# Second products of a block inversion four at a time, low-rank low parts padded to 128 rows, and another order of parts, in a two-layer hybrid backbone

## The chip, the cores and the metric

The kernel runs on one core of one Trainium2 chip. The metric is the time of one execution on the device in microseconds, as a median of several runs. Profiles come from one execution of the same program under the hardware profiler.

## The reference

Two layers work on 256 context tokens and 256 latent tokens of width 1024. Each layer has three token mixers fed by one projection (a bidirectional RWKV-7 recurrence, a bidirectional gated linear recurrence, neighbourhood attention), a merge by sigmoid gates, and a gated feed-forward part with a small convolution. What the change touches is the recurrence of the first mixer and the low-rank maps that feed it:

```python
w_lo = jnp.tanh(w_lo)
for d in range(2):
    w_log = -jax.nn.softplus(-(p['rwkv_w0'][d] + w_lo @ p['rwkv_w_up'][d])) - 0.5
    a = jax.nn.sigmoid(p['rwkv_a0'][d] + a_lo @ p['rwkv_a_up'][d])
...
def step(S, inp):
    r_t, w_t, k_t, v_t, kk_t, a_t = inp
    sa = jnp.einsum('bhvk,bhk->bhv', S, -kk_t)
    S = (S * w_t[:, :, None, :] + sa[..., None] * (kk_t * a_t)[:, :, None, :]
         + v_t[..., None] * k_t[:, :, None, :])
    return S, jnp.einsum('bhvk,bhk->bhv', S, r_t)
```

`w_lo` and `a_lo` have 64 columns each, and there are 16 heads of 64. In layer 1, the last, only the 256 latent tokens are needed after the recurrences, so most of its projections have 256 columns where layer 0 has 512.

## The kernel before

Activations lie transposed, channels on the 128 partitions and tokens on the free axis. A dense product (`mm3`, L247 to L249) splits weight and activation into a high part in fp32r and a low part, and adds three matmuls per 128-row block: high x high, high x low, low x high. A weight tile (`wload`) is fetched from memory as wr by SyncE's queue, rounded to wh by ScalarE (L226), and its low part wl is made by VectorE or GpSimd (L229); which of the two is read from a list of zeros and ones for each kind of projection (`lo` in the table CFG). One projection of 1024 inputs is 24 matmuls. They appear as pj (input projection), pbr, wo (merge), fg, fu, fo (feed-forward). All other matmuls are in fp32 and leave two records each in the trace.

The recurrence is computed in chunks of 64 tokens, for a pair of heads at a time, eight pairs p per layer. For each pair: `rw_key` makes k, v, r and the row norms (kst, then kbc), and splits the low-rank weights lw into lh and ll; `rw_prep` forms the decay and the gate by two products each, pw and pa, where lh has 128 rows and ll is applied with 64 (L511, L512, L518, L519); `rw_gram` forms 32 matrices of 64x64 in Gm (2 directions, 8 chunks, 2 heads); `rw_rows` transposes what the recurrence needs (vt, bt); `rw_inv` inverts the two 32x32 diagonal blocks of all 32 triangular matrices by substitution on VectorE (31 steps, L660 and L662, on the tile AT); `rw_inv2` makes the remaining block of each inverse by two products, Q (L681: one 32x32 matmul for each of the 32 matrices, then a ScalarE copy per half, L682) and Q2 (L687, named Q in the trace too, then L688), and then sends part of KR into Gm by DMA; `rw_seq` walks through the eight chunks (r, sa, sp, yp, with small copies by ScalarE, VectorE and GpSimd between them); `rw_out` and `rw_out2` normalise and store, the latter in one product for all tokens or in two halves (`oy` in CFG).

```python
for g in range(2):
    ps = self.ps("q", "Q2").rearrange("p (j t) -> p j t", t=32)
    for i in range(16):
        j = 16 * g + i
        nc.tensor.matmul(ps[64:96, i, :], lhsT=T1[96:128, j, :], rhs=TT[32:64, j, 32:64], start=True, stop=True)
    nc.scalar.activation(TT[0:32, 16 * g:16 * g + 16, 32:64], ps[64:96], AF.Copy)
```

The other two mixers (`lru_*`, `attn_*`) and the gate projections (`gate`) are independent of the recurrence and are laid between its steps. The order is given by CFG, one table per layer: `order` is a string with a letter for each part of one pair (g gram, i inversion, I second part of it, v rows, o and O output, X, a, b, Y, S the linear recurrence, Q, A, P attention, 1 and 2 key and prep of the next pair, T the walk through the chunks, G one gate projection, N further ones by the list `ng`), `pri` gives parts a priority, and `sp` places the attention's steps behind marked matmuls of projections. A scheduler then puts instructions into each engine's queue by program order and these priorities; each engine takes its queue in that order.

Of the kernel before, what the change touches and what calls it, by code (L numbers as in the profile page):

```python
# [10 lines left out]
F32 = mybir.dt.float32  # L11
F32R = mybir.dt.float32r
AF = mybir.ActivationFunctionType
ALU = mybir.AluOpType
# [5 lines left out]
P = 128  # L20
# [24 lines left out]
for _n, _c in _CS:  # L45
# [6 lines left out]


CFG = [{'f1': 0,
  'ff': [40000, 12000],
  'fg': 0,
  'fi': 20000,
  'hp': 10000,
  'lo': {'1': [0],
         'G': [0, 1],  # L60
         'N': [1, 0],
         'Q': [0],
         'X': [0],
         'Y': [0, 1, 0],
         'fi': [0],
         'fo': [1, 1, 1, 0],
         'fp': [0, 1, 0],
         'm0': [0, 1],
         'm1': [0, 0, 0, 0, 1, 1],
         'st': [1],  # L70
         'wo': [0]},
  'lq': 0,
  'mb': 8,
  'na': 0,
  'nb': 0,
  'nc': 3,
  'ng': [4, 1, 1, 2, 1, 0, 2, 0, 5],
  'no': 5,
  'order': '||g|ovOiXQIa||YbGSTA|12NPB|',
  'oy': 1,  # L80
  'pe': [0, 0, 0, 0, 0, 0, 0],
  'pri': {'1': 20000,
          '2': 5000,
          'B': 400,
          'O': 5000,
          'S': 10000,
          'T': 5000,
          'a': 5000,
          'g': 1200,
          'i': 20000,  # L90
          'o': -200,
          'v': 2500},
  'prs': 0,
  'rot': 1,
  'rv': 1,
  'rw': 0,
  'sp': [0, 0, 0.04, 0.05, 0.18, 0.4, 0.59, 0.92, 0.98],
  'sq': 0,
  'st': -1,
  'sw': 1,  # L100
  'wo': [0, 25000],
  'yo': 0},
 {'f1': 0,
  'ff': [300, 600],
  'fg': 6,
  'fi': 0,
  'hp': 20000,
  'lo': {'1': [0],
         'G': [0, 1],
         'N': [0],  # L110
         'Q': [0],
         'X': [1],
         'Y': [0],
         'fi': [0, 1, 1, 0, 1],
         'fo': [0],
         'fp': [0, 0, 1, 0],
         'm0': [0],
         'm1': [0, 1, 0, 0],
         'st': [0],
         'wo': [0]},  # L120
  'lq': 0,
  'mb': 4,
  'na': 2,
  'nb': 2,
  'nc': 2,
  'ng': [7, 1, 1, 1, 1, 1, 2, 0, 2],
  'no': 5,
  'order': 'gvGiIXabYSQA12TNPoOB',
  'oy': 1,
  'pe': [0, 0, 3, 0, 0, 0, 0],  # L130
  'pri': {'1': 20000,
          '2': 10000,
          'A': -200,
          'B': 20000,
          'I': 20000,
          'N': 20000,
          'O': 20000,
          'S': 0,
          'T': 20000,
          'Y': -200,  # L140
          'b': 200,
          'g': 20000,
          'i': 20000,
          'o': 20000,
          'v': 20000},
  'prs': 0,
  'rot': 0,
  'rv': 0,
  'rw': 1,
  'sp': [0.04, 0.43, 0.47, 0.47, 0.72],  # L150
  'sq': 0,
  'st': -1,
  'sw': 0,
  'wo': [25000, 15000],
  'yo': 1}]
STEP1 = [3, 2, 1, 0, 7, 6, 5, 4]

# [1 line left out]
class Net:  # L159
# [302 lines left out]
    def rw_key(self, R, Q, p, n0):  # L462
        nc = self.nc
        T2 = self.rw_t2(R, Q)
        lw = self.wp.tile([P, 1024], F32, tag="wr", name="lw", bufs=3)[:, :640]
        nc.sync.dma_start(lw, self.ins["lora"][self.l, p])
        lh = Q.tile([P, 512], F32R, tag="lh", name="lh")
        ll = Q.tile([P, 512], F32R, tag="ll", name="ll")
        self.split(lw[:, :512], lh, ll)
        gw = R.tile([P, P], F32, tag="gw", name="gw", bufs=2)  # L470
        nc.gpsimd.tensor_copy(gw, lw[:, 512:])
        k = T2("k")
        self.shift(self.proj(8 + p), 8 + p, k, 0)
        v = T2("v")
        self.shift(self.proj(16 + p), 16 + p, v, 0)
        r = T2("r")
        self.shift(self.proj(p, n0), p, r, n0)

        sq = T2("ta")
        nc.scalar.activation(sq, k, AF.Square, scale=self.pvc("kk", p))  # L480
        st = self.ps("g", "kst")
        for T in range(4):
            nc.tensor.matmul(st[:, 2 * T:2 * T + 2], lhsT=sq[:, T * P:(T + 1) * P], rhs=self.c["hsel"],
                             start=True, stop=True)
        n1 = R.tile([P, 8], F32, tag="n1", name="n1")
        nc.vector.tensor_scalar(n1, st[:, 0:8], 1e-24, None, op0=ALU.max)
        n2 = R.tile([P, 8], F32, tag="n2", name="n2")
        nc.gpsimd.tensor_tensor(n2, n1, self.mhalf[:, 0:8], op=ALU.pow)
        pn = self.ps("g", "kbc")
        nb = T2("th")  # L490
        nc.scalar.activation(nb.rearrange("p (g v) -> p g v", v=64),
                             n2.rearrange("p (g o) -> p g o", o=1).to_broadcast([P, 8, 64]), AF.Copy)
        for T in range(4):
            nc.tensor.transpose(pn[:, T * P:(T + 1) * P], nb[:, T * P:(T + 1) * P], self.ident)
        kk = T2("kk")
        nc.vector.scalar_tensor_tensor(kk, k, self.pvc("kk", p), pn, op0=ALU.mult, op1=ALU.mult)
        return dict(p=p, lh=lh, ll=ll, k=k, kk=kk, gw=gw, v=v, r=r)

    def rw_prep(self, R, Q, u, n0):
        nc = self.nc  # L500
        T2 = self.rw_t2(R, Q)
        p, lh, ll, k, kk, r = (u[n] for n in ("p", "lh", "ll", "k", "kk", "r"))
# [5 lines left out]
        for d in range(2):  # L508
            pw = self.ps("g", "pw")
            dc = slice(d * P, (d + 1) * P)  # L510
            nc.tensor.matmul(pw, lhsT=lh[:, dc], rhs=self.wS, start=True, stop=False)  # L511
            nc.tensor.matmul(pw, lhsT=ll[0:64, dc], rhs=self.wS[0:64], start=False, stop=True)  # L512
            th = T2("th")
            nc.scalar.activation(th, pw, AF.Tanh, scale=0.5, bias=self.hw0[:, 8 * d + p:8 * d + p + 1])
            nc.scalar.activation(th, th, AF.Copy, bias=1.0)
            pa = self.ps("g", "pa")
            dc = slice((2 + d) * P, (3 + d) * P)
            nc.tensor.matmul(pa, lhsT=lh[:, dc], rhs=self.aS, start=True, stop=False)  # L518
            nc.tensor.matmul(pa, lhsT=ll[64:128, dc], rhs=self.aS[64:128], start=False, stop=True)  # L519
            ta = T2("ta")  # L520
            nc.scalar.activation(ta, pa, AF.Tanh, scale=0.5, bias=self.hw0[:, 16 + 8 * d + p:16 + 8 * d + p + 1])
            G = T2("G")
# [144 lines left out]
    def rw_inv2(self, R, u):  # L667
        nc = self.nc
        G = u["Gm"]
        A10, A0, Ap, Tf = u["inv"]  # L670
        TT = u["TT"] = u["RT"][64:128].rearrange("p (j t) -> p j t", t=64)
        T1 = Ap
        nc.gpsimd.memset(TT[32:64, :, 0:32], 0.0)
        nc.vector.transpose(T1[0:32].rearrange("p j s -> p s j"), Tf[64:96].rearrange("p t s -> p s t"))
        nc.vector.transpose(TT[0:32, :, 0:32].rearrange("p j t -> p t j"), Tf[64:96])
        nc.vector.transpose(TT[32:64, :, 32:64].rearrange("p j t -> p t j"), Tf[96:128])
        for g in range(2):
            ps = self.ps("q", "Q").rearrange("p (j t) -> p j t", t=32)
            for i in range(16):
                j = 16 * g + i  # L680
                nc.tensor.matmul(ps[96:128, i, :], lhsT=A10[:, j], rhs=T1[0:32, j, :], start=True, stop=True)  # L681
            nc.scalar.activation(T1[96:128, 16 * g:16 * g + 16, :], ps[96:128], AF.Copy, scale=-1.0)  # L682
        for g in range(2):
            ps = self.ps("q", "Q2").rearrange("p (j t) -> p j t", t=32)
            for i in range(16):
                j = 16 * g + i
                nc.tensor.matmul(ps[64:96, i, :], lhsT=T1[96:128, j, :], rhs=TT[32:64, j, 32:64], start=True, stop=True)  # L687
            nc.scalar.activation(TT[0:32, 16 * g:16 * g + 16, 32:64], ps[64:96], AF.Copy)  # L688
        if not self.cfg['f1']:
            for h in range(2):  # L690
                nc.sync.dma_start(G[0:64, 0, :, :, h], u["KR"][64 * h:64 * h + 64, 0])
# [912 lines left out]
```

## Time and profile before

| what | value |
|---|---|
| median of 3 runs | 2999.29 us (2991.41 to 3010.68) |
| the profiled execution | 2999.59 us |
| its span, first to last instruction | 2997.8 us |
| mean granted TensorE clock | 0.957 |
| TensorE, VectorE, ScalarE, GpSimd busy | 2834.2, 1964.5, 1512.0, 595.7 us |

A busy time is the union of an engine's instructions. Matmuls overlap one another in the trace, so TensorE's pace is read from the starts of successive matmuls, and its clock from the column of the granted clock, where 1.00 is 2.4 GHz and 0.50 is 1.2 GHz. In time, the mixers of layer 0 take about 80 to 1030 us, merge and feed-forward follow to 1740 us, the mixers of layer 1 reach to 2660 us, and merge and feed-forward of layer 1 end the span.

### The profile page before, as it was taken

The numbers are of one execution on the slowest core, as the hardware profiler recorded it, in microseconds if no ns is written. First come the engines' busy times: TensorE is split into PE (matmuls) and PEld (weight loads), VectorE is DVE, ScalarE is ACT, GpSimd is POOL, SyncE is SP. The second block draws the span as 40 slices with busy tenths as digits, with TensorE's granted clock in tenths as the row PEclk, the third lists the DMA queues.
The fourth block names the chain that finished last, engine by engine and source line by source line (L and its number), as shares of the span: only waits on it lengthen the run. The fifth ranks groups of instructions, "written<-read, shape, count | busy, mean of one in ns | idle before, by whom it ended". The sixth has DMA issues, their size and how long they took to land. (4 is left out here: it accounts for less than half of the span.)

```text
span 2997.8 us, 51813 instructions
## 1 busy us (share of the span) xinstructions
PE 2834.2 (95%) x20144; PEld 2263.7 (76%) x20144; DVE 1964.5 (66%) x3947; ACT 1512.0 (50%) x2917; POOL 595.7 (20%) x618
## 2 busy tenths in 40 slices
PE   7999999999999999989999998999999999989998
PEld 5777777777767677787778887777777777678898
DVE  6768777677776744475443268687778768755774
ACT  3565554556546542353333356655655665634453
POOL 2121120211202212200002211222221221212440
PEclk9999999999999999999999999999999998979899
DMA  6322122221222345755653452222222222236663
GB/s 226 94 70 74 56 89 64 72 68 53 87 69 68 106 158 182 255 184 182 218 175 92 121 172 83 65 78 77 67 72 82 64 64 78 87 104 211 219 195 115
DMA packets 159222, 344.30 MB, mean 115 GB/s; under 512 B 47488, under 2 KB 74368, under 8 KB 158976
## 3 DMA queue, kind: packets, MB, share of 16 engines
q1 hardware_dynamic: 152064, 334.69, 34.8%
q10 hardware_dynamic: 6912, 6.29, 0.7%
q8 instruction: 159, 2.61, 0.4%
q14 instruction: 87, 0.71, 0.1%
HBM read 301.08 MB, written 25.17 MB: 109 GB/s over the span
## 5 line engine op out<-in xcount | busy, mean ns | idle before, releaser
L226 ACT ACTIVATE wh<-wr 128x1024 fp32r<-128x1024 f32 (+1 forms) x402 | 420.1, 1046 | 537.4 <-PE pj L248 195.1
L247 PE MATMUL pj<-hh,wh 128*128 128x512 f32 (+1 forms) x1440 | 561.4, 391 | 22.6 <-DVE k L432 14.7
L229 DVE TENSOR_TENSOR wl<-wr,wh 128x1024 fp32r<-128x1024 f32 (+1 forms) x320 | 411.2, 1285 | 250.8 <-ACT wh L226 240.4
L249 PE MATMUL pj<-hh,wl 128*128 128x512 f32 (+1 forms) x1440 | 551.7, 384 | 8.2 <-POOL wl L229 4.1
L248 PE MATMUL pj<-hl,wh 128*128 128x512 f32 (+1 forms) x1440 | 551.3, 383 | 0.0
L247 PEld LDWEIGHTS pj<-hh,wh 128*128 128x128 f32 x1440 | 282.7, 196 | 83.0 <-issue 24.9
L249 PEld LDWEIGHTS pj<-hh,wl 128*128 128x128 f32 x1440 | 282.7, 197 | 61.8 <-issue 8.8
L229 POOL TENSOR_TENSOR wl<-wr,wh 128x1024 fp32r<-128x1024 f32 (+1 forms) x82 | 199.0, 2429 | 629.9 <-ACT wh L226 602.7
L248 PEld LDWEIGHTS pj<-hl,wh 128*128 128x128 f32 x1440 | 283.2, 197 | 47.1 <-issue 8.9
L741 POOL TENSOR_TENSOR sg<-SV,gC 64x128 f32<-64x128 f32 x192 | 114.3, 595 | 337.3 <-DVE SV L756 272.6
L660 DVE TENSOR_TENSOR itmp<-AT 128x126 f32<-128x126 f32 (+22 forms) x496 | 140.0, 282 | 11.2
L662 DVE TENSOR_TENSOR AT<-AT,itmp 128x126 f32<-128x126 f32 (+22 forms) x496 | 134.7, 272 | 10.8
L586 PEld LDWEIGHTS gram<-KR,BK 64*128 64x128 f32 x1024 | 120.5, 196 | 26.3 <-issue 13.9
L586 PE MATMUL gram<-KR,BK 64*128 64x128 f32 (+1 forms) x1024 | 136.6, 290 | 0.9 <-DVE Gm L589 0.4
L247 PE MATMUL fo<-fh,wh 128*128 128x256 f32 (+1 forms) x418 | 130.3, 312 | 0.0
L249 PE MATMUL fo<-fh,wl 128*128 128x256 f32 (+1 forms) x418 | 130.2, 311 | 0.0
L248 PE MATMUL fo<-fl,wh 128*128 128x256 f32 (+1 forms) x418 | 129.8, 310 | 0.0
L247 PE MATMUL fg<-hh,wh 128*128 128x256 f32 (+1 forms) x384 | 128.2, 336 | 1.1 <-ACT hh L403 1.1
L247 PE MATMUL fu<-hh,wh 128*128 128x256 f32 (+1 forms) x384 | 125.3, 327 | 2.7 <-DVE fgs L1356 2.0
L248 PE MATMUL fg<-hl,wh 128*128 128x256 f32 (+1 forms) x384 | 126.8, 331 | 0.0
L249 PE MATMUL fg<-hh,wl 128*128 128x256 f32 (+1 forms) x384 | 126.5, 330 | 0.0
L249 PE MATMUL fu<-hh,wl 128*128 128x256 f32 (+1 forms) x384 | 125.5, 328 | 1.0 <-DVE wl L229 1.0
(337 smaller groups left out, 6321.0 us busy)
## 6 DMA issues: line engine op xcount, KB each, us to landing
wr<-in_w_in SPq DMA_DIRECT2D x180, 512.0 KB, 3.3
aw<-in_ada_w SPq DMA_DIRECT2D x96, 512.0 KB, 4.6
wr<-in_ffn_w_in SPq DMA_DIRECT2D x96, 512.0 KB, 4.1
wr<-in_w_branch SPq DMA_DIRECT2D x48, 512.0 KB, 3.6
wr<-in_ffn_w_out SPq DMA_DIRECT2D x36, 512.0 KB, 3.6
wr<-in_w_out SPq DMA_DIRECT2D x24, 512.0 KB, 4.7
Gm<-KR SPq DMA_DIRECT2D x32, 256.0 KB, 4.3
wr<-in_ffn_w_out SPq DMA_DIRECT2D x18, 384.0 KB, 3.1
```

Source lines behind the costliest of these rows:

```text
L226: nc.scalar.activation(hi, raw, AF.Copy)
L229: eng.tensor_tensor(lo, raw, hi.bitcast(F32), op=ALU.subtract)
L247: nc.tensor.matmul(o, lhsT=a, rhs=xh[k][:, n0:n1], start=(first and k == 0), stop=False)
L248: nc.tensor.matmul(o, lhsT=a, rhs=xl[k][:, n0:n1], start=False, stop=False)
L249: m = nc.tensor.matmul(o, lhsT=b, rhs=xh[k][:, n0:n1], start=False, stop=(last and k == kt - 1))
L586: nc.tensor.matmul(ps[:, i, 0:nx], lhsT=BK[hs, d, c, :], rhs=KR[hs, 0:nx, d, c, :], start=True, stop=True)
L660: eng.tensor_tensor(tmp, Ap[:, q + 1:32, q:q + 1].to_broadcast([P, nt, ns]), Tf[:, q:q + 1, 0:2 * ns:2].to_broadcast([P, nt, ns]), op=ALU. ...
L662: eng.tensor_tensor(Tf[:, q + 1:32, 0:2 * ns:2], Tf[:, q + 1:32, 0:2 * ns:2], tmp, op=ALU.subtract)
L741: nc.gpsimd.tensor_tensor(sg[64 * h:64 * h + 64], SV[0:64, i, :, h], gC[:, :, h, i:i + 1].to_broadcast([64, 2, 64]), op=ALU.mult)
```

## The change

Three pieces of code and both tables change. The second products take four of the 32 matrices at once: the four blocks of T1 stand side by side as one stationary operand of 128 columns, the four right-hand blocks as one moving operand of 128 columns, and of the sixteen 32x32 products that come out, the four on the diagonal are copied, each by a ScalarE instruction of its own for every fourth matrix. The low parts ll are made for the 64 rows that count in each half and set to zero in the others, and are applied with all 128 rows. The tables get another order of parts, other priorities, other lists of who makes wl, and other counts of gate projections per pair (`ng` counts them at the start and behind each pair's walk; the total stays 24 per layer).

```diff
 CFG = [{'f1': 0,
...
-  'ng': [4, 1, 1, 2, 1, 0, 2, 0, 5],
+  'ng': [3, 1, 3, 2, 1, 0, 2, 0, 4],
   'no': 5,
-  'order': '||g|ovOiXQIa||YbGSTA|12NPB|',
-  'oy': 1,
+  'order': 'g||ovOXiQ||a||Yb|IGAT|12|NSPB|',
+  'oy': 0,
...
  {'f1': 0,
...
-         'fi': [0, 1, 1, 0, 1],
-         'fo': [0],
+         'fi': [1],
+         'fo': [1],
...
-  'order': 'gvGiIXabYSQA12TNPoOB',
+  'order': 'GgviXabYISQA12TPNoOB',
...
@@ rw_key
-        self.split(lw[:, :512], lh, ll)
+
+        nc.scalar.activation(lh, lw[:, :512], AF.Copy)
+        for x in range(2):
+            rs, cs = slice(64 * x, 64 * x + 64), slice(256 * x, 256 * x + 256)
+            nc.vector.tensor_tensor(ll[rs, cs], lw[rs, cs], lh[rs, cs].bitcast(F32), op=ALU.subtract)
+            nc.gpsimd.memset(ll[rs, 256 - 256 * x:512 - 256 * x].bitcast(F32), 0.0)
@@ rw_prep
-            nc.tensor.matmul(pw, lhsT=ll[0:64, dc], rhs=self.wS[0:64], start=False, stop=True)
+            nc.tensor.matmul(pw, lhsT=ll[:, dc], rhs=self.wS, start=False, stop=True)
...
-            nc.tensor.matmul(pa, lhsT=ll[64:128, dc], rhs=self.aS[64:128], start=False, stop=True)
+            nc.tensor.matmul(pa, lhsT=ll[:, dc], rhs=self.aS, start=False, stop=True)
@@ rw_inv2
-            ps = self.ps("q", "Q2").rearrange("p (j t) -> p j t", t=32)
-            for i in range(16):
-                j = 16 * g + i
-                nc.tensor.matmul(ps[64:96, i, :], lhsT=T1[96:128, j, :], rhs=TT[32:64, j, 32:64], start=True, stop=True)
-            nc.scalar.activation(TT[0:32, 16 * g:16 * g + 16, 32:64], ps[64:96], AF.Copy)
+            ps = self.ps("q", "Q2").rearrange("p (m a t) -> p m a t", a=4, t=32)
+            for m in range(4):
+                j = slice(16 * g + 4 * m, 16 * g + 4 * m + 4)
+                nc.tensor.matmul(ps[:, m], lhsT=T1[96:128, j, :].rearrange("p a t -> p (a t)"), rhs=TT[32:64, j, 32:64],
+                                 start=True, stop=True)
+            for a in range(4):
+                nc.scalar.activation(TT[0:32, 16 * g + a:16 * g + 16:4, 32:64], ps[32 * a:32 * a + 32, :, a], AF.Copy)
```

On TensorE, around the inversion of the second pair of layer 0, the order before is this (the last row begins a projection whose 24 matmuls follow; L855 and L856 are products of the linear recurrence):

```order
L247 MATMUL pj_2578<-hh_368,wh 128x512
L681 MATMUL Q<-AT,Gm 32x32 x32
L248 MATMUL pj_2578<-hl_376,wh 128x512
L249 MATMUL pj_2578<-hh_368,wl 128x512
L855 MATMUL lr<-xb,gw 128x512
L856 MATMUL li<-xb,gw 128x512
L687 MATMUL Q_2527<-RT,AT 32x32 x16
L687 MATMUL Q_2545<-RT,AT 32x32 x16
L247 MATMUL pj_2624<-hh_361,wh 128x512
L247 MATMUL pj_2916<-hh_361,wh 128x512
```

In the changed kernel, at the same pair, the rows around the first products and those around the second are these, and the 23 projection matmuls between the two pieces are not shown:

```order
L252 MATMUL pj_2450<-hh_368,wl 128x512
L865 MATMUL lr<-xb,gw 128x512
L866 MATMUL li<-xb,gw 128x512
L689 MATMUL Q<-AT,Gm 32x32 x32
L250 MATMUL pj_2556<-hh_361,wh 128x512
L250 MATMUL pj_2837<-hh_361,wh 128x512
...
L252 MATMUL pj_2837<-hh_368,wl 128x512
L695 MATMUL Q_2536<-RT,AT 128x128 x4
L695 MATMUL Q_2545<-RT,AT 128x128 x4
L251 MATMUL pj_2556<-hl_369,wh 128x512
```

The two products of the linear recurrence have moved ahead of the first products, and 25 projection matmuls stand between the first and the second products where there were two and the pair lr, li.

At the last inversion of layer 1, TensorE's order before has attention ahead of it and the merge behind it:

```order
L1080 MATMUL ao<-PT,vt 64x64 x8
L681 MATMUL Q<-AT,Gm 32x32 x32
L687 MATMUL Q_25026<-RT,AT 32x32 x16
L687 MATMUL Q_25044<-RT,AT 32x32 x16
L723 MATMUL r_25310<-SV,Gm 128x128 x2
```

The changed kernel has the same neighbours there:

```order
L1090 MATMUL ao<-PT,vt 64x64 x8
L689 MATMUL Q<-AT,Gm 32x32 x32
L695 MATMUL Q_24872<-RT,AT 128x128 x4
L695 MATMUL Q_24881<-RT,AT 128x128 x4
L733 MATMUL r_25038<-SV,Gm 128x128 x2
```

Nothing has moved into this place; only the form of the second products differs.

GpSimd's queue ends so before, with the row norm of the last residual (st_r) behind 25 weight halves:

```order
L1128 TENSOR_TENSOR M_25683<-M_25683,mth 128x256
L229 TENSOR_TENSOR wl<-wr,wh 128x1024
L276 TENSOR_TENSOR st_r<-st_m,mhalf 128x2 x2
L229 TENSOR_TENSOR wl<-wr,wh 128x1024 x25
L276 TENSOR_TENSOR st_r<-st_m,mhalf 128x2
```

In the changed kernel it ends so, with three more groups of 4 and 2 rows like the third and fourth from the end left out:

```order
L232 TENSOR_TENSOR wl<-wr,wh 128x1024 x2
L279 TENSOR_TENSOR st_r<-st_m,mhalf 128x2 x2
L232 TENSOR_TENSOR wl<-wr,wh 128x1024 x45
...
L232 TENSOR_TENSOR wl<-wr,wh 128x1024 x4
L232 TENSOR_TENSOR wl<-wr,wh 128x768 x2
L232 TENSOR_TENSOR wl<-wr,wh 128x1024
L279 TENSOR_TENSOR st_r<-st_m,mhalf 128x2
```

All 68 weight halves of layer 1's feed-forward part stand on GpSimd, and VectorE's queue has none of them.

## Rows read from the trace of the kernel before

**Rows 1.** The page's first part: busy time, share, instructions of each engine.
```profile
PE 2834.2 (95%) x20144; PEld 2263.7 (76%) x20144; DVE 1964.5 (66%) x3947; ACT 1512.0 (50%) x2917; POOL 595.7 (20%) x618
```
**Rows 2.** Busy time of each engine by stage, with granted clock and DMA.
```profile
core 0: us, PE busy (x) PEld busy (x) DVE busy (x) ACT busy (x) POOL busy (x), PEclk, DMA share, GB/s
80.00:1030.00 950.00, 925.51 (x6278) 688.69 (x6277) 704.01 (x1531) 533.10 (x1103) 183.62 (x224) 0.97 0.24 74
1740.00:2600.00 860.00, 805.37 (x5802) 632.06 (x5801) 640.34 (x1357) 512.20 (x1042) 191.48 (x246) 0.95 0.26 79
2600.00:2660.00 60.00, 45.50 (x350) 35.70 (x349) 41.34 (x115) 24.06 (x58) 5.06 (x5) 0.69 0.32 97
```
**Rows 3.** What TensorE waited for: us in total, times, longest us.
```profile
PE Q L681 <- DVE AT L674: 18.1, 12, 4.8
PE kbc L494 <- ACT th L491: 13.6, 13, 2.3
PE r L723 <- DMA Gm<-KR: 2.3, 1, 2.3
```
**Rows 4.** TensorE's timeline in layer 0: start us, us, instruction.
```profile
187.84 0.40 PE L248 MATMUL pj<-hl,wh 128*128 128x512 f32 x1
188.07 0.40 PE L518 MATMUL pa<-aS,lh 128*128 128x512 f32 x1
188.40 0.50 PE L519 MATMUL pa<-aS,ll 64*128 64x512 f32 x1
188.83 0.51 PE L249 MATMUL pj<-hh,wl 128*128 128x512 f32 x1
189.17 0.40 PE L247 MATMUL pj<-hh,wh 128*128 128x512 f32 x1
189.41 0.40 PE L248 MATMUL pj<-hl,wh 128*128 128x512 f32 x1
189.73 0.56 PE L745 MATMUL sa<-r,RT 64*64 64x64 f32 x6
190.22 0.50 PE L249 MATMUL pj<-hh,wl 128*128 128x512 f32 x1
190.56 0.39 PE L247 MATMUL pj<-hh,wh 128*128 128x512 f32 x1
```
**Rows 5.** Instructions on pw, pa, lh and ll: ns min/median/max, first and last start.
```profile
L511 PE MATMUL pw<-wS,lh x32: 388/404/628, 74.2 to 2527.1; 128*128 128x512 f32 x32
L512 PE MATMUL pw<-wS,ll x32: 491/498/792, 74.5 to 2527.5; 64*128 64x512 f32 x32
L518 PE MATMUL pa<-aS,lh x32: 387/397/632, 76.0 to 2540.0; 128*128 128x512 f32 x32
L519 PE MATMUL pa<-aS,ll x32: 491/497/792, 76.3 to 2540.4; 64*128 64x512 f32 x32
L237 DVE TENSOR_TENSOR ll<-lw,lh 128x512 fp32r<-128x512 f32 x16 | 11.0, 685 | 2.0 <-ACT lh L234 1.9
```
**Rows 6.** A GpSimd group by form: busy us, mean ns, idle before.
```profile
L709 POOL MEMSET SV<- 64x256 f32 x16 | 4.9, 308 | 7.3 <-PE yp L706 6.6 <-DVE pr L917 0.6
```
**Rows 7.** TensorE's timeline: second products at full and half clock, gram.
```profile
2101.92 2.21 PE L687 MATMUL Q<-RT,AT 32*32 32x32 f32 x64
...
1994.15 3.62 PE L687 MATMUL Q<-RT,AT 32*32 32x32 f32 x64
...
222.71 2.05 PE L586 MATMUL gram<-KR,BK 64*128 64x128 f32 x16
```
**Rows 8.** Stretches around one inversion; granted clock is the third from last.
```profile
1989.40:1991.50 2.10, 2.10 (x65) 2.09 (x64) 2.09 (x2) 0.77 (x2) 0.00 (x0) 1.00 0.00 0
1992.10:1994.10 2.00, 2.00 (x11) 1.82 (x9) 1.97 (x2) 0.20 (x2) 0.00 (x0) 0.51 0.42 86
1994.20:1997.60 3.40, 3.40 (x65) 3.40 (x64) 2.89 (x6) 1.49 (x2) 0.00 (x0) 0.50 0.51 104
```
**Rows 9.** ScalarE's copies out of Q2 and of r.
```profile
L688 ACT ACTIVATE RT<-Q x32: 567/587/597, 148.7 to 2644.4; 32x512 f32<-32x512 f32 x32
...
L728 ACT ACTIVATE r<-r 64x128 f32<-64x128 f32 x256 | 69.2, 270 | 74.2 <-PE r L723 68.8 <-ACT wh L226 0.2
```
**Rows 10.** The last inversion: TensorE's first products and their wait.
```profile
2636.85 3.61 PE L681 MATMUL Q<-AT,Gm 32*32 32x32 f32 x64 [4.75 <-DVE AT L674]
```
**Rows 11.** GpSimd's weight halves in layer 1's feed-forward part.
```profile
2817.63 3.16 POOL L229 TENSOR_TENSOR wl<-wr,wh 128x1024 fp32r<-128x1024 f32 x1 [0.18 <-ACT wh L226]
2854.05 2.41 POOL L229 TENSOR_TENSOR wl<-wr,wh 128x1024 fp32r<-128x1024 f32 x1 [5.92 <-DVE fgs L1355]
```
**Rows 12.** TensorE's timeline in layer 1's feed-forward part, 256 columns.
```profile
2839.64 0.28 PE L247 MATMUL fu<-hh,wh 128*128 128x256 f32 x1
...
2841.04 0.28 PE L247 MATMUL fu<-hh,wh 128*128 128x256 f32 x1
```
**Rows 13.** DMA issues: KB each, median us from issue to landing.
```profile
Gm<-KR SPq DMA_DIRECT2D x32, 256.0 KB, 4.3
```

More of the change, by code (lines that the diff above doesn't have):

```diff
@@ L54 @@
 CFG = [{'f1': 0,
-  'ff': [40000, 12000],
+  'ff': [40000, 0],
   'fg': 0,
-  'fi': 20000,
-  'hp': 10000,
+  'fi': 10000,
+  'hp': 20000,
   'lo': {'1': [0],
-         'G': [0, 1],
-         'N': [1, 0],
+         'G': [0, 1, 1],
+         'N': [0],
          'Q': [0],
          'X': [0],
-         'Y': [0, 1, 0],
+         'Y': [0, 0, 1, 0, 1, 0],
          'fi': [0],
-         'fo': [1, 1, 1, 0],
+         'fo': [1, 0, 1],
          'fp': [0, 1, 0],
-         'm0': [0, 1],
-         'm1': [0, 0, 0, 0, 1, 1],
-         'st': [1],
+         'm0': [1],
+         'm1': [0, 0, 1, 1],
+         'st': [1, 0],
          'wo': [0]},
   'lq': 0,
-  'mb': 8,
+  'mb': 4,
   'na': 0,
@@ L83 @@
           '2': 5000,
-          'B': 400,
+          'B': 2500,
           'O': 5000,
+          'P': 400,
           'S': 10000,
           'T': 5000,
-          'a': 5000,
+          'a': 400,
+          'b': 0,
           'g': 1200,
@@ L91 @@
           'o': -200,
-          'v': 2500},
+          'v': 20000},
   'prs': 0,
@@ L96 @@
   'rw': 0,
-  'sp': [0, 0, 0.04, 0.05, 0.18, 0.4, 0.59, 0.92, 0.98],
+  'sp': [0, 0, 0.16, 0.23, 0.24, 0.47, 0.6, 0.83, 1],
   'sq': 0,
@@ L101 @@
   'wo': [0, 25000],
-  'yo': 0},
+  'yo': 1},
  {'f1': 0,
@@ L106 @@
   'fi': 0,
-  'hp': 20000,
+  'hp': 10000,
   'lo': {'1': [0],
@@ L110 @@
          'N': [0],
-         'Q': [0],
+         'Q': [0, 0, 0, 0, 0, 1],
          'X': [1],
          'Y': [0],
-         'fi': [0, 1, 1, 0, 1],
-         'fo': [0],
-         'fp': [0, 0, 1, 0],
-         'm0': [0],
-         'm1': [0, 1, 0, 0],
+         'fi': [1],
+         'fo': [1],
+         'fp': [1, 0, 0, 0, 0, 0],
+         'm0': [0, 0, 1, 1, 1, 0],
+         'm1': [0],
          'st': [0],
@@ L122 @@
   'mb': 4,
-  'na': 2,
+  'na': 1,
   'nb': 2,
@@ L126 @@
   'ng': [7, 1, 1, 1, 1, 1, 2, 0, 2],
-  'no': 5,
-  'order': 'gvGiIXabYSQA12TNPoOB',
+  'no': 4,
+  'order': 'GgviXabYISQA12TPNoOB',
   'oy': 1,
   'pe': [0, 0, 3, 0, 0, 0, 0],
-  'pri': {'1': 20000,
-          '2': 10000,
+  'pri': {'1': 2500,
+          '2': 200,
           'A': -200,
-          'B': 20000,
+          'B': -200,
           'I': 20000,
-          'N': 20000,
+          'N': 400,
           'O': 20000,
@@ L140 @@
           'Y': -200,
-          'b': 200,
+          'a': 0,
+          'b': 2500,
           'g': 20000,
-          'i': 20000,
+          'i': 5000,
           'o': 20000,
-          'v': 20000},
+          'v': 200},
   'prs': 0,
@@ L149 @@
   'rw': 1,
-  'sp': [0.04, 0.43, 0.47, 0.47, 0.72],
+  'sp': [0.0, 0.35, 0.36, 0.55, 0.64],
   'sq': 0,
-  'st': -1,
+  'st': -2,
   'sw': 0,
-  'wo': [25000, 15000],
+  'wo': [600, 15000],
   'yo': 1}]
```

## Prediction

> **What bounds the kernel now.** I read the page first. TensorE has matmuls in flight 95% of the span, VectorE is busy 66%, ScalarE 50%, GpSimd 20% [rows 1]. The table by stage says the same of each: TensorE is 97% busy in the mixers of layer 0 (80 to 1030 us) and 94% in those of layer 1 (1740 to 2600 us); the one poor stretch is 2600 to 2660 us, 45.5 us of 60 at a mean clock of 0.69 [rows 2]. So a change pays through what TensorE issues, what it waits for, and the clock it is granted. The waits come next: the longest sum of any one cause is 18.1 us, in front of the first products of the inversion (Q, L681), for VectorE's transposes [rows 3]. The last view is the timeline, for the spacing of starts. In a run of whole-array matmuls of 512 columns one starts every 0.23 us. A matmul that uses part of the array breaks that: in rows 4 the 64-row product L519 starts 0.33 us after L518, its successor L249 0.43 us later, and the next L247 0.34 us after that. Durations hide this, since matmuls overlap; starts show it.
>
> The profiled execution took 2999.59 us, its span 2997.8, 1.8 us outside it. The median of the three runs is 2999.29 us, so the sum is made against 2999.6.
>
> **The padded low parts.** 64 matmuls (2 layers, 8 pairs of heads, 2 directions, two kinds) lose their 64-row form. The trace has them at 498 and 497 ns, against 404 and 397 ns for the 128-row products before them [rows 5]. From rows 4, each costs 0.33 + 0.43 + 0.34 = 1.10 us over three starts, where three whole-array starts cost 3 x 0.235 = 0.70: 0.40 us too much. Where the next matmul is itself of part of the array (nearly one in six of them), about half of that stays. That is 64 x 0.40 = 25.6 us at most; at one third of the gain, the excess of the 64-row start alone (0.20 x 64), 13. I take **-22 us**, with -13 to -26 as the ends. A rule of the Trainium skill speaks against this term (TensorE: Matmul & The Clock Gate, "Why this matters for your kernels"): a single 32-row matmul takes as long as one with 128 rows. By it the term is 0; the durations in rows 5 do not agree. What makes the padding: one VectorE subtract of 685 ns [rows 5] becomes two over 64x256, and GpSimd gets two memsets of 64x256, 308 ns each in the row of that size [rows 6]. In the new order both stand a whole pair ahead of the products that read them, right behind the last readers of the old content. VectorE has a third of its time free; I cost them at nothing. Without that cover it would be 16 x 0.6 = 10 us.
>
> **The second products.** Per inversion 32 products of 32x32 (64 records) become 8 of 32x128 by 128 columns (16 records). The block of 64 records lasts 2.21 us in the timeline at full clock and 3.62 us at half [rows 7]. The nearest row of the new size is the gram product, 64 rows, 128 columns: 16 records in 2.05 us [rows 7]. So 0.16 x 16 = **-3 us**; at half clock the new block would be twice as long, 0.2 us worse than the old, so the ends are 0 and -3 from work alone.
>
> What the clock adds is a term of its own. The first block (at 1989.4) runs at 1.00; behind it the granted clock falls to its lower level, 1.2 GHz, and the projections and the second block in this case run at 0.51 and 0.50 [rows 8]. Five of the 16 second blocks lie wholly there, and 1.4 us (3.62 less 2.21) comes back for each that leaves it: 7 us. The new blocks fill four times the columns of the array, and in layer 0 a projection separates them from the first block; the first block is untouched. I take **-7 us**, from 0 to -36 (the last end is a rival).
>
> The results now leave PSUM by four ScalarE copies per half in place of one. One took about 0.59 us [rows 9]; four of 128 elements, at the 270 ns of the nearest row (L728, 64x128) [rows 9], are 1.08. That is 32 x 0.49 = 16 us more of ScalarE. In layer 0, seven projection matmuls and r lie between the last second product and sa, which needs the result, about 2 us; that covers it. In the last inversion nothing lies between, but there r waits for the transfer into Gm anyhow (2.3 us, [rows 3]). I take **+1 us**; with all cover gone it is +16.
>
> **The order.** In layer 0 one more projection (24 matmuls, 24 x 0.23 = 5.5 us) now stands ahead of the first products of most inversions, and 25 matmuls between the two blocks where there were as few as two. VectorE meanwhile has 89 to 96 instruction rows from the first transpose of an inversion to the last in most pairs, where it had 93 to 104. Of the 18.1 us in rows 3, 4.75 us are the last inversion's [rows 10], whose place is unchanged. The other 13 can go; something is late elsewhere, first of all the row norm (kbc waits for ScalarE's th, 13.6 us [rows 3]), whose cover in layer 1 shrinks in places from five matmuls to two. I take **-12 us**; the ends are -19 and, as a rival, a loss.
>
> TensorE's sequence goes from whole array to part of it 491 times, before 526; 64 of the 526 were the low parts, so without them the count rises by 29. One such visit costs: from 189.41 to 190.56 us two whole starts and six sa records took 1.15 us; 0.47 are the two starts and 6 x 0.059 the records, which leaves 0.33 [rows 4]. 29 x 0.33 = 9.6 us; direct changes between two kinds of part-array products fall from 270 to 217, which gives some back. **+5 us** (0 to +10). The last inversion of layer 1 leaves TensorE idle a quarter of 2600 to 2660 us [rows 2], and 24 more projection matmuls of 256 columns move into it: 24 x 0.12 = **-3 us** (0 to -3).
>
> All 68 low halves of layer 1's weights in the feed-forward part go to GpSimd (before 26 of the 44 of the first two products and none of the last one's). One takes 2.41 us there [rows 11]; TensorE uses a weight in 2.8 us (twelve of its 24 matmuls take 1.40 [rows 12]). So TensorE stays the later one and I cost it at nothing; if each took 3.16, the longest in rows 11, it would be 68 x 0.35 = +24 us. One output product instead of two halves in layer 0 (rw_out2) streams the same columns; nothing, or up to -4. DMAs: the transfer into Gm, 4.3 us to landing [rows 13], still has over 6 us of matmuls between its release (the first products) and r everywhere but in the last inversion, as before.
>
> Sum: -22 - 3 - 7 + 1 - 12 + 5 - 3 = -41, so 2999.6 - 41 = **2958 us** after rounding down.
>
> **The rivals.** *The padding gives nothing*, as the skill's rule has it: 2958 + 22 = 2980. For it: the longer duration may be the change of rows, paid anyway at a neighbour. Against it: in rows 4 both neighbours are whole-array.
> *The order gives nothing*: waits only change their place, the two blocks stay slow, and the 29 visits cost in full: -22 - 3 + 1 + 10 = -14, so 2986. For it: before, TensorE was already 97% busy in layer 0.
> *The clock*: means of 0.97 and 0.95 over 950 and 860 us [rows 2] are 71 us of full-speed work lost; if the wide blocks bring back half, it is -36 in place of -7: 2929. Against it: the first blocks stay as they are, and the clock falls behind these.
> *The inversion comes late* (slower): VectorE carries eleven more weight halves in layer 0's mixers, which GpSimd did before, and in layer 1 the first products stand earlier in the sequence, ahead of a low-rank product. If each of the 16 waits became like the last one, 4.75 us [rows 10], they would sum to 76 us, 58 more than now, and the result is 2958 + 12 + 58 = 3028. It decides against the change once these waits pass 18 + 29 = 47 us, 2.9 per inversion. Against it: the longer cover ahead of the first products in layer 0.
>
> **How the numbers follow.** The forecast has 0.62, with 2938 to 2978 as its own range; padding for nothing 0.10, order for nothing 0.12, clock 0.08, late inversion 0.08. A measurement of this kernel tells about 1% from no change, so the bounds are 2969 and 3029. Faster: 0.85 of the forecast, the clock, a little of the order's case, 0.63. Slower: half of the late inversion, 0.04. Same: 0.33. The range, 2918 to 2992, leaves out the late inversion and the tails.
>
> **What would show it.** Right: the low products of pw and pa last 0.40 us and start 0.23 us apart; sixteen-record blocks of Q2 near 2.05 us; the wait for L674's successor under 8 us; a mean clock of 0.96 to 0.97. Wrong: low products that still start 0.33 us or more behind their partner; waits of sa for the copies out of Q2, or of the feed-forward matmuls for GpSimd's wl, of over 5 us; a first block that waits more than 2.9 us for VectorE each time; or a clock that rises by more than 0.015.

## The result, and the profile after

The changed kernel took 2970.09 us (median of three runs, 2964.05 to 2974.57) against 2999.29; the ratio on record is 0.9888 (95% interval 0.9853 to 0.9922), a little under the quotient of the two medians, 0.990. In six more runs beside other kernels it took 2977.19 us against 3001.78, a ratio of 0.9920 (0.9898 to 0.9942). By the medians that is 29 and 25 us less, by the ratios 34 and 24; the forecast was 41 less. Both times lie inside the likeliest case's own range of 2938 to 2978, at its upper end. The bound for faster, 2969 us, was just missed by both medians, although the first ratio lies more than 1% under 1.

The page's first part of the changed kernel, the execution of 2964.05 us, answers to [rows 1]:

```profile
span 2962.2 us, 50439 instructions
PE 2784.8 (94%) x19360; PEld 2241.2 (76%) x19360; DVE 1941.1 (66%) x3921; ACT 1521.7 (51%) x3005; POOL 694.0 (23%) x676
```

The table by stage, with the columns of [rows 2] (granted clock third from last), of the same execution:

```profile
80.00:1030.00 950.00, 917.67 (x6082) 691.41 (x6083) 725.88 (x1583) 544.84 (x1171) 177.72 (x231) 0.99 0.26 77
1740.00:2600.00 860.00, 794.27 (x5398) 621.64 (x5396) 648.27 (x1426) 520.99 (x1097) 199.06 (x254) 0.94 0.26 76
2600.00:2660.00 60.00, 52.39 (x459) 47.07 (x460) 31.93 (x67) 24.93 (x59) 8.66 (x14) 0.84 0.43 122
```

The gain is not spread over the span. The merge of layer 0 ends its mixers; its first matmul starts at 1087.3 us before and at 1056.0 after, 31 us sooner. From there to the end the span has 1910.5 us before and 1906.2 after: in these two profiles all but 4 us of the gain was made in the mixers of layer 0, where the granted clock rose from 0.97 to 0.99 (0.02 x 950 = 19 us of full-speed work). A second profile of the changed kernel, from the six later runs, has the merge 26 us sooner and gives 11 of them back behind it. The rows of the first two starts, from before and after:

```profile
L247 PE MATMUL pbr<-hh,wh x128: 388/389/795, 1087.3 to 1245.3; 128*128 128x512 f32 x128
```

```profile
L250 PE MATMUL pbr<-hh,wh x128: 387/390/796, 1056.0 to 1216.3; 128*128 128x512 f32 x128
```

What TensorE waited for after the change (us in total, times, longest), against [rows 3]:

```profile
PE kbc L502 <- ACT th L499: 15.3, 15, 2.1
PE Q L689 <- DVE AT L682: 10.2, 6, 5.0
PE r L733 <- DVE SV L766: 5.4, 14, 0.6
PE sa L755 <- ACT r L738: 3.3, 9, 1.4
PE pj L252 <- POOL wl L232: 1.7, 1, 1.7
PE r L733 <- DMA Gm<-KR: 1.4, 1, 1.4
PE fg L252 <- POOL wl L232: 0.9, 1, 0.9
PE fu L252 <- POOL wl L232: 0.6, 1, 0.6
```

The wait ahead of the first products fell by 8 us, and small waits of the walk (r for SV, 14 times; sa for r's copy) took the place of some of it. In all, waits alone explain little of 30 us.

The padded products start 0.24 us behind their partner and 0.22 us ahead of the next, where [rows 4] had 0.33 and 0.43:

```profile
172.03 0.40 PE L250 MATMUL pj<-hh,wh 128*128 128x512 f32 x1
172.26 0.39 PE L526 MATMUL pa<-aS,lh 128*128 128x512 f32 x1
172.50 0.39 PE L527 MATMUL pa<-aS,ll 128*128 128x512 f32 x1
172.72 0.39 PE L251 MATMUL pj<-hl,wh 128*128 128x512 f32 x1
172.95 0.39 PE L252 MATMUL pj<-hh,wl 128*128 128x512 f32 x1
```

The durations of the groups that the change touched, with the columns of [rows 5]:

```profile
L520 PE MATMUL pw<-wS,ll x32: 387/394/628, 73.4 to 2487.0; 128*128 128x512 f32 x32
L527 PE MATMUL pa<-aS,ll x32: 389/396/662, 75.0 to 2498.8; 128*128 128x512 f32 x32
L476 DVE TENSOR_TENSOR ll<-lw,lh x32: 407/421/500, 43.1 to 2419.2; 64x256 fp32r<-64x256 f32 x32
L477 POOL MEMSET ll<- x32: 302/306/428, 36.4 to 2397.4; 64x256 f32 x32
L698 ACT ACTIVATE RT<-Q x128: 264/267/274, 146.5 to 2613.1; 32x128 f32<-32x128 f32 x128
```

And one inversion of layer 0 in TensorE's timeline, then the last one of layer 1 at half clock (compare [rows 7, 10]):

```profile
255.25 2.21 PE L689 MATMUL Q<-AT,Gm 32*32 32x32 f32 x64
263.60 2.05 PE L695 MATMUL Q<-RT,AT 32*128 32x128 f32 x16
...
2604.59 3.62 PE L689 MATMUL Q<-AT,Gm 32*32 32x32 f32 x64 [5.01 <-DVE AT L682]
2608.53 3.75 PE L695 MATMUL Q<-RT,AT 32*128 32x128 f32 x16 [0.32 <-DVE RT L684]
```

The wide block takes 2.05 us, as the gram row had said, and 3.75 at half clock, 0.13 more than the narrow one: the prices of the instructions were right. Whether the pieces were worth what the sum gave them needs the experiments.

### The profile page after: what moved, and what is told of

It is laid out like the page before. It is cut to its first block, busy times and chain, and to the rows that moved or that the text cites. A ratio compares the mean times of both kernels' runs of the same rounds, so it can differ in the third digit from the quotient of the medians.

```text
span 2962.2 us, 50439 instructions
## 1 busy us (share of the span) xinstructions
PE 2784.8 (94%) x19360; PEld 2241.2 (76%) x19360; DVE 1941.1 (66%) x3921; ACT 1521.7 (51%) x3005; POOL 694.0 (23%) x676
## 5 line engine op out<-in xcount | busy, mean ns | idle before, releaser
L232 DVE TENSOR_TENSOR wl<-wr,wh 128x1024 fp32r<-128x1024 f32 (+1 forms) x286 | 359.3, 1257 | 212.0 <-ACT wh L229 186.7
L232 POOL TENSOR_TENSOR wl<-wr,wh 128x1024 fp32r<-128x1024 f32 (+1 forms) x116 | 273.5, 2366 | 537.1 <-ACT wh L229 527.2
L751 POOL TENSOR_TENSOR sg<-SV,gC 64x128 f32<-64x128 f32 x192 | 121.4, 632 | 331.4 <-DVE SV L766 267.2
L594 PEld LDWEIGHTS gram<-KR,BK 64*128 64x128 f32 x1024 | 117.5, 193 | 24.4 <-issue 10.2
L766 DVE TENSOR_TENSOR SV<-sp,sg 64x128 f32<-64x128 f32 x192 | 55.2, 288 | 118.8 <-PE sp L761 114.9
```

Source lines behind the costliest of these rows:

```text
L232: eng.tensor_tensor(lo, raw, hi.bitcast(F32), op=ALU.subtract)
L594: nc.tensor.matmul(ps[:, i, 0:nx], lhsT=BK[hs, d, c, :], rhs=KR[hs, 0:nx, d, c, :], start=True, stop=True)
L751: nc.gpsimd.tensor_tensor(sg[64 * h:64 * h + 64], SV[0:64, i, :, h], gC[:, :, h, i:i + 1].to_broadcast([64, 2, 64]), op=ALU.mult)
L766: nc.vector.tensor_tensor(SV[0:64, i + 1, :, h], pp[hs, :, h], sg[hs], op=ALU.add)
```

## The experiments

The change has three pieces: padding, wide second products, tables. Two kinds of kernel take them apart. In the first kind the scheduler is free, as in both kernels. That turned out to matter: padding leaves 98% or more of TensorE's sequence (counted by kind of product over the traces) as it was, while the wide products alone, with the old tables, leave 82%; the scheduler has 24 matmuls fewer and six copies more per inversion to place, and lays everything behind them otherwise. So in the second kind ("order held") every engine's sequence is fixed to that of a named kernel by edges that set the order of issue on each engine. No run holds a kernel to its own order, so what the holding costs by itself was not measured; in the pairs compared below, the held kernel is once the one with wide products and twice the one with narrow ones.

All results in one table. The kernels ran in three series, each on another chip and each with the kernel before; the difference is (ratio - 1) x the median of before in the same series (3001.3, 3003.9 and 3001.8 us). The medians alone would move a difference by up to 5 us.

| kernel | padding | products | tables, order | ratio to before (95%) | us |
|---|---|---|---|---|---|
| padding alone | yes | narrow | old | 0.9944 (0.9923 to 0.9964) | -17 |
| wide alone | no | wide | old | 1.0048 (1.0026 to 1.0071) | +14 |
| both codes | yes | wide | old | 1.0011 (0.9988 to 1.0034) | +3 |
| tables alone | no | narrow | new, free | 1.0012 (0.9987 to 1.0037) | +4 |
| wide, order held | no | wide | old, before's order | 1.0009 (0.9988 to 1.0030) | +3 |
| without padding | no | wide | new | 0.9949 (0.9929 to 0.9969) | -15 |
| order alone | no | narrow | new, changed kernel's order | 0.9909 (0.9887 to 0.9932) | -27 |
| narrow, order held | yes | narrow | new, changed kernel's order | 0.9879 (0.9852 to 0.9907) | -36 |
| table of layer 0 | yes | narrow | new in layer 0, old in 1 | 0.9885 (0.9858 to 0.9912) | -35 |
| one copy | yes | wide, one copy | new, changed kernel's order | 0.9893 (0.9869 to 0.9917) | -32 |
| filled wait | yes | narrow | new, changed kernel's order | 0.9872 (0.9846 to 0.9899) | -38 |
| changed kernel again | yes | wide | new | 0.9920 (0.9898 to 0.9942) | -24 |

**Padding alone.** The kernel before with this edit and the making of ll from the change:

```diff
-            nc.tensor.matmul(pw, lhsT=ll[0:64, dc], rhs=self.wS[0:64], start=False, stop=True)
+            nc.tensor.matmul(pw, lhsT=ll[:, dc], rhs=self.wS, start=False, stop=True)
...
-            nc.tensor.matmul(pa, lhsT=ll[64:128, dc], rhs=self.aS[64:128], start=False, stop=True)
+            nc.tensor.matmul(pa, lhsT=ll[:, dc], rhs=self.aS, start=False, stop=True)
```

> Before, with the padded low parts alone (old tables, narrow second products). Theory: 64 matmuls each take 0.40 us less of TensorE over three starts, about half of it in each layer: 13 to 26 us less, most likely 22, so 2977 us; the low products of pw and pa last 0.40 us. Rival, the padding gives nothing because a 64-row product costs as much as a 128-row one: 2999 us. Second rival, the gain comes back as waits because VectorE's chain of the inversion is no faster: between the two, 2985 to 2995, with the wait of Q for AT longer than 18 us.

Measured: 17 us less. TensorE's timeline of this kernel, near the place of [rows 4]:

```profile
185.62 0.40 PE L522 MATMUL pa<-aS,lh 128*128 128x512 f32 x1
185.86 0.39 PE L523 MATMUL pa<-aS,ll 128*128 128x512 f32 x1
186.09 0.40 PE L249 MATMUL pj<-hh,wl 128*128 128x512 f32 x1
186.32 0.39 PE L247 MATMUL pj<-hh,wh 128*128 128x512 f32 x1
```

Over the low products at full clock (60 of the 64 in each trace), the three steps around one, from its partner's start to that of its second successor, sum to 1.03 us on average before and to 0.74 here: 64 x 0.29 = 19 us. Timing and starts agree, so the rival "padding gives nothing" is out. The rule of the Trainium skill behind that rival (TensorE: Matmul & The Clock Gate, "Why this matters for your kernels") is given for a single 32-row matmul; for the 64-row products here, which stand among other matmuls, the trace does not agree (0.50 us long, padded 0.40). The waits ahead of the first products rose from 18.1 to 21.0 us in total, which is the second rival's sign, but small beside the gain.

**Wide products alone**, and **both pieces of code**, with the old tables and a free scheduler. The edit is that of the change in `rw_inv2`; the second adds the padding.

> Before, with the second products four at a time alone. Theory: 3 us less of work, up to 7 less through the clock, 1 more through the copies: 2990 us, at the edge of what can be told. Rival, the narrow second blocks bring much of the low clock: 36 less, 2963 us, and the time at the lower clock level falls by half. Rival on the other side, the four copies per half stand on the path (sa waits for ScalarE): 16 more, 3012 us or over 2999 in any case.

> Before, with both pieces of code (padding and wide second products) and the old tables. If the terms add: 22 + 3 + 7 - 1 = 31 less, 2968 us, which is where the changed kernel lies already, and then the new tables gave nothing. By the prediction's sum the tables are worth 10 more, so this kernel should lie 10 above the changed one, near 2980 where the changed kernel is at 2970. Rival: the new code only pays with the new tables, and this kernel stays above 2990.

Measured: +14 and +3 us. With the old tables and a free scheduler, the wide products take back what the padding gives. For the wide products alone, 3010.72 us is near the slow rival's 3012, but its sign did not come: sa's waits for ScalarE's copies of r are 1.2 us in all, 0.8 before. For both pieces the rival's number came: with the old tables the new code gives nothing.

**Tables alone.**

> The changed kernel's tables with the old code (low parts of 64 rows, narrow second products). Theory: order -12, whole-to-part visits +5, projections into the end of the mixers -3: 2989 us. Rival, the tables were fitted to the new code and alone give nothing or a loss: 2999 us or more. Rival, the tables carry most of the result because the shorter waits ahead of the first products and the clock of layer 0 come from the order: 2975 us, with layer 0's mixers 20 us or more shorter than before and layer 1's not.

Measured: +4 us, the number of the first rival; but the second rival's sign is there too. The mixers of layer 0 end 27 us sooner than before's (the merge's first matmul starts at 1060.0 us), and from there on this execution takes 45 us longer than before's. Its last inversion comes late, and the granted clock in layer 1's mixers is 0.90 where before had 0.95. Its timeline, its waits and that stage:

```profile
2657.58 3.59 PE L685 MATMUL Q<-AT,Gm 32*32 32x32 f32 x64 [13.73 <-DVE AT L678]
```

```profile
PE Q L685 <- DVE AT L678: 23.8, 8, 13.7
1740.00:2600.00 860.00, 807.51 (x5516) 631.32 (x5514) 618.05 (x1321) 497.43 (x1009) 190.47 (x236) 0.90 0.24 74
```

The late inversion is the prediction's slower rival at one place, and explains 9 of the 45 us (13.7 against 4.75 [rows 10]). The clock is the larger part: 0.05 x 860 = 43 us of full-speed work. Why it is lower is not shown, and the profiled execution was the slowest of this kernel's twelve (3017.09 us, median 3004.72). The scheduler, given narrow products, made another order of the same table: 72% of TensorE's sequence, counted as above, is that of the changed kernel.

**The order held.** The remaining kernels answer what each piece does when nothing else moves. The edit, beside the undone pieces:

```diff
+def hold(tc, nc):
+    want = json.loads(zlib.decompress(base64.b64decode(HELD)))
+    for e, v in _traced(nc).items():
...
+        for a, b in zip(seq, seq[1:]):
+            tc.add_manual_dep(b, a.name, mybir.DependencyInfo(mybir.DependencyClass.NoSync, mybir.DependencyReason.DATA), reason="held")
```

HELD is the list of places of a kernel's instructions on each engine. Where a group of four narrow products stands for one wide product, it takes that one's place, and one copy takes the place of the last of four.

> The changed kernel with the low parts back to 64 rows; its order of instructions stays nearly the same. Theory: the padding is worth here what it was worth in the old kernel, 17 to 22 us: 2987 to 2992 us, low products at 0.50 us again. Rival: part of the padding's gain in the old kernel was the granted clock and it gives half here: about 2978.

> The changed kernel with the narrow second products (32 products and one copy per half), every engine's order held to that of the changed kernel by issue-order edges, so that only the products differ. By the prediction's terms (-3 work, -7 clock, +1 copies) this is 9 us above the changed kernel: 2979. Rival: the wide products themselves are worth nothing, all of the difference came by the order that the scheduler made around them: 2970. Rival: the wide products hold the clock up: 2990 or more, with the time at the lower level up by 40 us.

> Before with the wide second products alone, every engine's order held to that of before by issue-order edges. If the 14 us that the wide products cost with the free scheduler came from the reshuffled order, this kernel is at or under before: 2990 to 2999 us (2991 by the prediction's terms). If they come from the products and their four copies themselves (copies on the path of sa), it stays at 3010.

> Before's code (low parts of 64 rows, narrow second products) with the new tables, its order held to the one the scheduler makes for the wide products. Theory: the order itself is worth 10 to 20 us, and the new tables alone gave nothing only because the scheduler made another order of them: 2980 to 2985 us. Rival: the order is worth nothing without the new code: 3000 to 3005, as with the new tables and a free scheduler. By the prediction's terms (-12 +5 -3) it is 2990.

Without padding (free, but over 99% of the sequence kept): -15 us (2985.35, between the two answers and nearer the first), where the changed kernel has -24 and -34, so padding is worth 9 to 19 here; between the two kernels with narrow products (-27, -36) it is 9. Wide products in before's order: +3 (3003.10, between the two answers), which can't be told from nothing. So 11 of the 14 us lost with the free scheduler would be its new order, although the two intervals overlap by a hair. In the changed kernel's order, narrow products are no slower than wide ones: 0.9879 against 0.9888 and 0.9920; without padding it is 0.9909 against 0.9949, intervals that overlap by a hair. Three pairs, none with a gain from the wide products. In the first the wide kernel is the held one, in the other two the narrow one, so neither a cost nor a benefit of holding can hide such a gain in all three. The expectation of 2979 for the narrow ones failed, at 2964.70.

The order alone gives 27 us, with before's code (2975.94 us, better than the 2980 to 2985 expected). Its stage, and its wait ahead of the first products:

```profile
80.00:1030.00 950.00, 919.06 (x6426) 686.03 (x6424) 726.62 (x1568) 535.25 (x1116) 172.35 (x216) 1.00 0.25 77
```

```profile
PE Q L719 <- DVE AT L712: 9.2, 6, 5.0
```

The clock in layer 0's mixers is 1.00 here, 0.97 before. This is not one execution's luck: in the five profiles with the old table of layer 0 it is 0.97 or 0.98, in the nine with the new one 0.98 once, 0.99 seven times and 1.00 once. What the order does to it is seen at one inversion of layer 0. Before, five stretches: projections, the wait, the first products, what follows, and the second products (columns of [rows 8]):

```profile
261.00:265.60 4.60, 4.60 (x22) 3.75 (x20) 4.33 (x14) 3.11 (x8) 0.00 (x0) 1.00 0.35 114
265.60:267.80 2.20, 0.43 (x3) 0.05 (x2) 2.13 (x3) 0.00 (x0) 0.00 (x0) 1.00 0.00 0
267.80:270.80 3.00, 3.00 (x64) 3.00 (x64) 2.99 (x2) 0.59 (x1) 0.00 (x0) 0.60 0.03 5
270.80:275.30 4.50, 4.50 (x9) 1.84 (x7) 1.99 (x2) 2.93 (x4) 0.00 (x0) 0.51 0.28 58
275.30:278.00 2.70, 2.70 (x67) 2.55 (x67) 0.00 (x0) 0.98 (x2) 0.31 (x1) 1.00 0.51 136
```

And the same pair in the changed kernel: projections with lr and li, the first products, a projection, the second products:

```profile
248.00:255.20 7.20, 7.20 (x29) 5.03 (x27) 7.05 (x6) 4.81 (x10) 0.00 (x0) 1.00 0.00 0
255.30:257.40 2.10, 2.10 (x66) 2.06 (x65) 2.10 (x4) 1.25 (x3) 0.00 (x0) 1.00 0.00 0
257.40:263.50 6.10, 6.09 (x27) 4.53 (x25) 2.60 (x4) 5.60 (x9) 0.62 (x1) 1.00 0.98 200
263.60:265.60 2.00, 2.00 (x18) 1.88 (x17) 2.00 (x2) 1.98 (x3) 0.56 (x1) 1.00 1.12 237
```

Before, TensorE stood still for 1.8 us and then did 64 records that use a 32x32 part of the array; the clock fell to 1.2 GHz inside that block, and the next 4.5 us, projections among them, ran at 0.51. After, the wait is covered and nothing falls. Of before's eight first blocks in layer 0, six stood more than 1.5 us behind their predecessor, and in five of these the clock fell within the block; the two others kept 1.00. In the order-alone kernel six of eight follow at once (0.52 us), and the clock fell within none of the eight (behind one of the two others it did). So the 1.8 us wait cost about 5: itself, and 3.0 x 0.40 + 4.5 x 0.49 = 3.4 for the work done at the lower clock behind it. As an estimate, five such falls are at most 17 us, and with the 9 us by which the waits shrank this is near the 27. The Trainium skill (TensorE: Matmul & The Clock Gate, "HAM oscillation — how this bites in real kernels") tells of such a second payment behind waits for transfers; the trace agrees that it is paid, and adds that here the clock still stood at 1.00 in the wait and fell in the block behind it (0.60).

It isn't a rule without exceptions. In [rows 8], from layer 1 before, the first block follows its predecessor after 0.21 us, and the clock falls behind it all the same; the one at 2097.57 us waited 1.45 us and the clock stayed at 1.00. And no run moves only lr and li ahead of the first products: that the covered wait, and not another part of layer 0's new table, steadies the clock is read from these traces and not tested by itself.

**The copies.**

```diff
             for a in range(4):
-                nc.scalar.activation(TT[0:32, 16 * g + a:16 * g + 16:4, 32:64], ps[32 * a:32 * a + 32, :, a], AF.Copy)
+                if a == 2:
+                    nc.scalar.activation(TT[0:32, 16 * g:16 * g + 16, 32:64], ps[64:96].rearrange("p m a t -> p (m a) t"), AF.Copy)
```

> The changed kernel in its own order, with one ScalarE copy per half of the second products in place of four; so the results of three of every four matrices are wrong entries, and 96 ScalarE instructions are left out. If the four copies cost what they add to ScalarE (0.49 us per half, 16 us in all), 2954; by the prediction's +1 it stays at 2969. If the kernel with narrow products is 5 us faster than the changed one because of the copies, this one is near 2964 too; if because of the wide matmuls, it stays at 2970.

Measured 2970.79 beside the changed kernel's 2977.19: between the answers for the copies and for the wide matmuls, with overlapping intervals. One wait agrees in kind: sa's for r's copy on ScalarE, 3.3 us in the changed kernel's first profile and 2.1 in its second, is 0.6 here and 0.7 with narrow products:

```profile
PE sa L793 <- ACT r L776: 0.6, 3, 0.2
```

What the four copies cost is thus some microseconds at most of the possible 16; how much, if anything, is open.

**The changed kernel again**, and **a filled wait.** The last edit adds, ahead of the last inversion's first products:

```diff
+            if g == 0 and len(UNITS) == 15:
+                for i in range(FILL):
+                    mm = nc.tensor.matmul(qp, lhsT=self.wS[:, :P], rhs=self.wS, start=True, stop=True)
```

> The changed kernel once more, for a tighter interval and beside the next three. Every theory: 2970 us, ratio to before 0.985 to 0.992.

> The kernel with the narrow second products in the changed kernel's order, with 16 extra matmuls of 128x512 that compute nothing needed in the last inversion's 5 us wait of TensorE for VectorE. They take 3.4 us at 2.4 GHz and 6.8 at 1.2. Theory: what TensorE did before sets the clock there, and with the wait filled the two blocks of that inversion run in 2.0 us in place of 3.4, and the walk behind them starts at 2.4 GHz: 3 to 8 us less than without the fill, 2957 to 2962. Rival: the clock there stays at its lower level whatever fills the wait, and the fill costs up to 2 us: 2965 to 2967.

Measured for the changed kernel: the 2977.19 us given above, a ratio of 0.9920, at the expectation's upper end. For the filled wait: 2965.09, against 2964.70 for the same kernel without the fill in another series: no difference that can be told. That is the rival's number, but not its mechanism. The timeline shows why, first without the fill, then with it:

```profile
2600.61 3.62 PE L723 MATMUL Q<-AT,Gm 32*32 32x32 f32 x64 [5.01 <-DVE AT L716]
2604.55 3.59 PE L729 MATMUL Q<-RT,AT 32*32 32x32 f32 x64 [0.32 <-DVE RT L718]
...
2598.29 4.77 PE L725 MATMUL Q<-wS 128*128 128x512 f32 x16
2603.52 2.21 PE L729 MATMUL Q<-AT,Gm 32*32 32x32 f32 x64 [0.47 <-DVE AT L717]
2607.46 3.59 PE L735 MATMUL Q<-RT,AT 32*32 32x32 f32 x64 [1.73 <-DVE RT L719]
```

The 16 extra matmuls took 4.77 us, and the first block did run at full clock (2.21 us, without the fill 3.62): at this one place only what TensorE did in the wait was changed, and the clock followed. But TensorE then waited 1.73 us for RT, where it had waited 0.32, and the second block was at half clock again. What the faster block gained was spent waiting for VectorE.

**The table of layer 0 alone**, with padding and narrow products:

> Before with the padded low parts, the new table for layer 0 and the old one for layer 1; second products narrow. Tables alone made the mixers of layer 0 27 us shorter and those of layer 1 56 us longer in the profile, and padding alone gave 17 to 20 us. If the table of layer 0 works without the wide products, the two add: 2999 - 27 - 17 = 2955 to 2965 us, under the changed kernel. Rival: the table of layer 0 needs the wide products, or the clock takes the gain back: 2975 to 2985.

Measured 2964.97 us, -35, at the upper end of the 2955 to 2965 expected. The table of layer 0 needs no wide products.

A version that beats both kernels is thus at hand: the new order or the new table of layer 0, the padding, and the old second products. In three kernels of this kind the ratios are 0.9872 to 0.9885. The filled one, in the same series as the changed kernel, was 12 us faster, with intervals (0.9846 to 0.9899 and 0.9898 to 0.9942) that only touch.

## Why the prediction was right, and where its sum was not

The time fell into the forecast's own range. The sum behind it was near in total by errors that cancel, which is luck: the order gave 17 us more than its three terms, the second products 12 to 21 less than theirs, the padding 3 to 13 less.

- **The padding, -22:** right in mechanism, somewhat large. 17 in the old order, 9 to 19 in the new one. "Nearly one in six" is right: in before's trace 9 of the 60 at full clock have a next matmul on part of the array. Too large is the 0.40 for the others: it was read where two 128x512 projection products follow, which holds for 15 of the 60, while 34 have among their next two a product that is not a projection's. The mean is 0.29. In the new order, held, the three steps fall from 1.00 to 0.68 us, 64 x 0.32 = 20 us, and 9 were measured; where the rest came back isn't settled. (Of the ends given, 0.20 a product is half of 0.40, not a third.)
- **The second products, -3, clock -7, copies +1:** wrong together. The block's length was right (2.05 us, at half clock 0.13 worse), but held in place the wide products gave between +3 and +12 us, never the -9 of these three terms. The failed step is "1.4 us comes back for each that leaves it": at an equal order the wide blocks don't keep the clock up. The mean granted clock in layer 0's mixers is 0.99 with wide and with narrow products in the changed kernel's order, and two wide second blocks of layer 1 still ran at half clock, one of them at 2608.53 us above. The rival "the clock", -36 from the wide blocks, falls with it. Whether they cost something, and if so whether it is the copies, isn't settled.
- **The order, -12, +5, -3:** 27 in place of 10. The wait ahead of the first products fell by 8 us of the 12 forecast. The failed step is to have priced a removed wait at its own length: in layer 0 before, five of the six longer waits were followed by a fall of the clock, and the work at half speed behind them cost more than the wait. The clock's gain was in the sum, but it stood at the wide blocks and not at the order. The +5 for visits and the -3 for the end of layer 1's mixers were not measured by themselves.
- **Layer 1** has half of the padded products, and no gain that can be told: behind layer 0's mixers one profile of the changed kernel is 4 us shorter than before, the other 11 longer, with clocks of 0.94 and 0.92 in layer 1's mixers where before had 0.95. But the six profiles with the old table of layer 1 range from 0.92 to 0.95 there, so these differences are within what that stage does by itself. Whether the new table of layer 1 gives or costs anything isn't settled; the kernel with the old one is as fast.
- **GpSimd's weight halves, 0:** right. The feed-forward matmuls waited 1.5 us for them. **Gm's DMA, 0:** right.
- Of the signs given ahead: 0.40 us and 0.23 apart, 2.05 us and a clock of 0.96 to 0.97 came (0.966; in the later profile 0.957, just under it); the wait of Q was 10.2 us, not under 8; none of the signs against came.
- The rival "the order gives nothing" is out by the order-alone kernel, and "the inversion comes late" didn't happen in the changed kernel, but did at one inversion, the last, in the one with its tables and the old code.

## What to carry to other kernels

Price a TensorE wait not at its length alone: look at the granted clock of the stretch behind it, here where products on a part of the array followed. Before crediting or blaming an edit in a scheduled kernel, compare the instruction order of all engines, and time the edit once with the order held; here one edit read +14 us free and +3 held, and one table +4 free and -27 held. Padding a 64-row contraction with zeros to all 128 rows, worth 9 to 19 us for 64 products here, is worth trying where such a product stands between whole-array ones.

## What the runs showed that was not expected

The granted clock differs between executions of one and the same kernel, and with it the time. Before ran 35 times in one series, from 2979.97 us at a mean clock of 0.965 to 3013.65 at 0.951; time and clock have a correlation of -0.95, and 0.01 of clock is worth 23 us. The two profiled executions of the changed kernel show it in layer 1's mixers, with the same instructions: 0.94 in the table at the top, 0.92 in the other one, whose span was 2982.9 us:

```profile
1740.00:2600.00 860.00, 803.77 (x5356) 635.80 (x5355) 634.00 (x1369) 515.72 (x1081) 197.95 (x256) 0.92 0.26 75
```

A single profile is therefore no ground for terms under some 10 us in a stretch whose clock isn't steady; the sum's own clock term was as small as that.
